# A 512-byte load put ahead of the first store of an interleaving copy kernel

## The chip, the cores and the metric

The kernel runs on one core of a Trainium2 chip. The metric is the device time of one execution in microseconds (us). Before the change its median over three runs is 314.22 us. Besides these runs there is one profiled execution, whose trace gives every instruction, the issue and landing of every transfer, and the packets of the core's 16 DMA engines.

## The reference: what is computed

Two float32 arrays `x` and `y` of shape (32, 256, 1024), 33.55 MB each, are woven together along the last axis into one array of shape (32, 256, 2048), 67.11 MB:

```python
result = np.zeros((batch, seq, dim * 2), dtype=np.float32)
result[..., 0::2] = x
result[..., 1::2] = y
```

There is no arithmetic. Every input byte is read from HBM once and every output byte is written to HBM once, 134.22 MB in all.

## The kernel before

All arrays are taken flat. With P = 128 partitions and W = 8192 elements, `x` and `y` fall into n = 8 steps of 128 x 8192 elements (4 MB each, 32 KB to a partition), and the output into 8 steps of 128 x 16384. Each output step is made and stored in two halves h = 0, 1 of 128 x 8192. There are two tiles each of `xt`, `yt` (input, by the parity of the step k) and `ot` (output, by the half h), 32 KB to a partition each.

Three engines share the work, each with an order written out by hand:

- **SP's queue (q1 in the profile) loads.** Line 45 loads the first half of x of step 0. After that it loads y of step 0 (line 55), then x (line 52) and y (line 55) of each following step. The loads of steps 0 and 1 wait for nothing. From step 2 on, a load waits until VectorE has read the tile that it overwrites (lines 50 and 54, the semaphore `woven`, which counts finished copies).
- **VectorE (DVE) weaves.** For each half, line 67 copies a half of `xt` into the even columns of `ot[h]`, and line 70 a half of `yt` into the odd columns. From step 1 on, line 66 makes it wait until the store that last read `ot[h]` has landed (`osem[h]`).
- **ACT's queue (q10) loads once and stores.** Line 46 loads the second half of x of step 0 (semaphore `hsem`). Lines 72 to 78 then store each half when both of its copies are done (line 74). A store moves 4 MB. The very first one is issued in two pieces of 1 MB and 3 MB (`parts`, with Q = W/4); both are counted by `osem[0]`, and line 66 waits for both before step 1.

`tile_interleave_kernel` also moves the first load of SP and of ACT (lines 45 and 46) to the front of the program, ahead of its opening barrier. At the end ACT waits for the last store of half 0 (line 80) and clears the semaphores in one range (line 83), and SP waits for the last store of half 1 (line 84). That last wait ends the span.

All loads of SP's queue and all stores of ACT's queue run on the same 16 DMA engines.

Of the kernel before, what the change touches and what calls it, by code (L numbers as in the profile page):

```python
# [3 lines left out]


def _interleave(nc, x, y, out):
    P = 128
    W = 8192
    H = W // 2  # L10

    total = 1
    for s in x.shape:
        total *= s
    n = total // (P * W)
    assert n * P * W == total

    def rows(ap, names, k):
        flat = ap.rearrange("b s d -> (b s d)")
        return flat[k * names : (k + 1) * names].rearrange("(p w) -> p w", p=P)  # L20

    fp32 = mybir.dt.float32
    xt = [nc.alloc_sbuf_tensor(f"xt{b}", [P, W], fp32).ap() for b in (0, 1)]
    yt = [nc.alloc_sbuf_tensor(f"yt{b}", [P, W], fp32).ap() for b in (0, 1)]
    ot = [nc.alloc_sbuf_tensor(f"ot{b}", [P, W], fp32).ap() for b in (0, 1)]

    xsem = [nc.alloc_semaphore(f"xsem{b}") for b in (0, 1)]
    hsem = nc.alloc_semaphore("hsem")
    ysem = [nc.alloc_semaphore(f"ysem{b}") for b in (0, 1)]
    woven = nc.alloc_semaphore("woven")  # L30
    osem = [nc.alloc_semaphore(f"osem{b}") for b in (0, 1)]

    xs = [rows(x, P * W, k) for k in range(n)]
    ys = [rows(y, P * W, k) for k in range(n)]
    os_ = [rows(out, 2 * P * W, k) for k in range(n)]

    Q = W // 4

    def parts(k, h):
        return [slice(0, W)] if k or h else [slice(0, Q), slice(Q, W)]  # L40

    def stored(k, h):
        return 16 * sum(len(parts(j, h)) for j in range(k))

    nc.sync.dma_start(out=xt[0][:, :H], in_=xs[0][:, :H]).then_inc(xsem[0], 16)
    nc.scalar.dma_start(out=xt[0][:, H:], in_=xs[0][:, H:]).then_inc(hsem, 16)
    for k in range(n):
        b = k % 2
        if k >= 2:
            nc.sync.wait_ge(woven, 4 * (k - 2) + 3)  # L50
        if k:
            nc.sync.dma_start(out=xt[b], in_=xs[k]).then_inc(xsem[b], 16)
        if k >= 2:
            nc.sync.wait_ge(woven, 4 * (k - 2) + 4)
        nc.sync.dma_start(out=yt[b], in_=ys[k]).then_inc(ysem[b], 16)

    for k in range(n):
        b = k % 2
        for h in (0, 1):
            c = slice(h * H, (h + 1) * H)  # L60
            if h == 0:
                nc.vector.wait_ge(xsem[b], 16 * (k // 2 + 1))
            elif k == 0:
                nc.vector.wait_ge(hsem, 16)
            if k:
                nc.vector.wait_ge(osem[h], stored(k, h))
            nc.vector.tensor_copy(out=ot[h][:, 0::2], in_=xt[b][:, c]).then_inc(woven, 1)  # L67
            if h == 0:
                nc.vector.wait_ge(ysem[b], 16 * (k // 2 + 1))
            nc.vector.tensor_copy(out=ot[h][:, 1::2], in_=yt[b][:, c]).then_inc(woven, 1)  # L70

    for k in range(n):
        for h in (0, 1):
            nc.scalar.wait_ge(woven, 4 * k + 2 * h + 2)
            for c in parts(k, h):
                nc.scalar.dma_start(
                    out=os_[k][:, h * W : (h + 1) * W][:, c], in_=ot[h][:, c]
                ).then_inc(osem[h], 16)

    nc.scalar.wait_ge(osem[0], stored(n, 0))  # L80
    used = sorted(s.num for s in [*xsem, hsem, *ysem, woven, osem[0]])
    assert used == list(range(used[0], used[-1] + 1)), used
    nc.scalar.sem_clear(range(used[0], used[-1] + 1))
    nc.sync.nop(nofuse=True).wait_op(osem[1], stored(n, 1), "sem-ge").then_inc(
        osem[1], -stored(n, 1)
    )


def kernel(tc, x, y, out):
    nc = tc.nc  # L90
    tc.close()
    tc.compile()

    _interleave(nc, x, y, out)

    blocks = nc.main_func.blocks
    for engine in (mybir.EngineType.SP, mybir.EngineType.Activation):
        opening = blocks[0].instructions
        at, moved = next(
            (b, i)  # L100
            for b in blocks[1:]
            for i in b.instructions
            if i.engine == engine and i.opcode == "DMACopy"
        )
        assert not (moved.sync_info and moved.sync_info.on_wait)
        body = at.instructions
        body.remove(moved)
        gate = next(
            n
            for n, i in enumerate(opening)  # L110
            if i.engine == engine and i.opcode == "Drain"
        )
        opening.insert(gate, moved)
        at.instructions = body
        blocks[0].instructions = opening


# [1 line left out]
_INS = ['x', 'y']  # L119
_OUTS = [((32, 256, 2048), 'float32')]  # L120


# [23 lines left out]
```

## Time and profile before

| What | Value |
|---|---|
| Runs before: median, lowest, highest | 314.22, 314.08, 314.38 us |
| Profiled execution: own time, span | 314.21 us, 312.9 us (312.88) |
| Bytes moved | 134.22 MB, mean 429 GB/s over the span |
| DMA packets' time, share of 16 engines' span | q1 48.5%, q10 51.3% |
| DVE busy | 71.9 us (23%), 32 copies of about 2.29 us |
| Load of y of step 0 landed | 22.00 us |
| First store issued, its two pieces landed | 24.35 us; 40.4 and 57.5 us |
| x and y of step 1 (issued at 1.95 and 2.48 us) landed | 32.9 and 46.9 us |
| Last store issued, landed | 298.04 us, 312.85 us |

The span runs from the first to the last instruction of the profiled execution. The execution's own time is 1.33 us longer, which lies around the span. Rates in the windows view are the bytes of the packets that start in a window, divided by its length; so a window gives a true rate only where it holds whole packets. TensorE does nothing here, and the columns of its clock can be passed over.

### The profile page before, as it was taken

To read this page: it belongs to the slowest core of one execution; us is meant where nothing else is said; L and a number is where in the kernel's file an instruction comes from. 1 tells how busy PE (TensorE), PEld (TensorE's weight loads), DVE (VectorE), ACT (ScalarE), POOL (GpSimd) and SP (SyncE) were. 2 spreads that over 40 slices of the span, in tenths; PEclk is the share of its full clock that TensorE was granted. 3 is DMA by queue.
4 is the path that set the end of the run, shared out by engine and by line. 5 is a ranking of instruction groups with operands and counts; after the bars stand their busy time and mean duration, and the time that the engine had idled before them with its cause. 6 is when DMAs were issued, how large, how long until landed. Compare 5 with 4: busy or idle time off the path is not lost.

```text
span 312.9 us, 114 instructions
## 1 busy us (share of the span) xinstructions
DVE 71.9 (23%) x32; POOL 0.2 (0%) x4
## 2 busy tenths in 40 slices
DVE  0216000501305023050230503205032050415400
POOL 0000000000000000000000000000000000000000
DMA  8999999999999999999999999999999999999998
GB/s 344 461 406 431 436 402 431 440 465 406 448 423 431 440 406 465 402 469 402 469 402 465 406 457 415 436 436 419 452 402 469 402 469 402 469 402 461 411 444 360
DMA packets 4896, 134.22 MB, mean 429 GB/s; under 512 B 544, under 2 KB 544, under 8 KB 544
## 3 DMA queue, kind: packets, MB, share of 16 engines
q10 hardware_dynamic: 2592, 69.21, 51.3%
q1 hardware_dynamic: 2304, 65.01, 48.5%
HBM read 67.11 MB, written 67.11 MB: 429 GB/s over the span
## 4 chain that ended last, share of the span: by engine, by line
DMA 82%; DVE 12%; issue 0%
DMA out_dram<-ot 76%; DMA yt<-in_y_dram 7%; DVE ot L70 6%; DVE ot L67 6%
## 5 line engine op out<-in xcount | busy, mean ns | idle before, releaser
L67 DVE COPY ot<-xt 128x4096 f32<-128x4096 f32 x16 | 36.7, 2295 | 218.0 <-DMA out_dram<-ot 206.3
L70 DVE COPY ot<-yt 128x4096 f32<-128x4096 f32 x16 | 36.6, 2288 | 8.0 <-DMA yt<-in_y_dram 8.0
L130 POOL MEMSET const-uint8-127<- 128x1 uint8 x1 | 0.1, 102 | 0.0
L130 POOL MEMSET const-bfloat16-1.0<- 128x1 bf16 x1 | 0.1, 101 | 0.0
L130 POOL MEMSET const-float32-0.0<- 128x1 f32 x1 | 0.1, 98 | 0.2 <-issue 0.2
L130 POOL MEMSET const-float32-1.0<- 128x1 f32 x1 | 0.1, 98 | 0.0
## 6 DMA issues: line engine op xcount, KB each, us to landing
out_dram<-ot ACTq DMA_DIRECT2D x15, 4096.0 KB, 34.1
yt<-in_y_dram SPq DMA_DIRECT2D x8, 4096.0 KB, 41.5
xt<-in_x_dram SPq DMA_DIRECT2D x7, 4096.0 KB, 24.4
out_dram<-ot ACTq DMA_DIRECT2D x1, 3072.0 KB, 32.8
xt<-in_x_dram SPq DMA_DIRECT2D x1, 2048.0 KB, 11.7
xt<-in_x_dram ACTq DMA_DIRECT2D x1, 2048.0 KB, 13.4
out_dram<-ot ACTq DMA_DIRECT2D x1, 1024.0 KB, 16.1
```

The lines of the kernel that those rows point to most:

```text
L67: nc.vector.tensor_copy(out=ot[h][:, 0::2], in_=xt[b][:, c]).then_inc(woven, 1)
L70: nc.vector.tensor_copy(out=ot[h][:, 1::2], in_=yt[b][:, c]).then_inc(woven, 1)
L130: nc = _bacc.Bacc("TRN2", target_bir_lowering=False, num_devices=1)
```

## The change

ACT issues one more DMA directly ahead of the first store, behind the same wait on `woven`. It loads 8 rows of 16 float32 (64 bytes each, 512 bytes in all) from step 0 of x into a new tile `spare`, which nothing reads. Its semaphore `tsem` is waited for after ACT's last store was issued, and it is cleared with the others.

```diff
+    spare = nc.alloc_sbuf_tensor("spare", [8, 16], fp32).ap()
...
     hsem = nc.alloc_semaphore("hsem")
+    tsem = nc.alloc_semaphore("tsem")
...
     for k in range(n):
         for h in (0, 1):
             nc.scalar.wait_ge(woven, 4 * k + 2 * h + 2)
+            if k == h == 0:
+                nc.scalar.dma_start(out=spare, in_=xs[0][:8, :16]).then_inc(tsem, 16)
             for c in parts(k, h):
                 nc.scalar.dma_start(
                     out=os_[k][:, h * W : (h + 1) * W][:, c], in_=ot[h][:, c]
                 ).then_inc(osem[h], 16)

+    nc.scalar.wait_ge(tsem, 16)
     nc.scalar.wait_ge(osem[0], stored(n, 0))
-    used = sorted(s.num for s in [*xsem, hsem, *ysem, woven, osem[0]])
+    used = sorted(s.num for s in [*xsem, hsem, tsem, *ysem, woven, osem[0]])
```

## The prediction

> **What bounds the kernel now.** I read the page first, for which resource is full.
>
> ```profile
> span 312.9 us, 114 instructions
> DVE 71.9 (23%) x32; POOL 0.2 (0%) x4
> DMA  8999999999999999999999999999999999999998
> q10 hardware_dynamic: 2592, 69.21, 51.3%
> q1 hardware_dynamic: 2304, 65.01, 48.5%
> ```
>
> The packets of the two queues fill 51.3 + 48.5 = 99.8% of the time of 16 DMA engines, and the third line has no slice below 8 tenths. VectorE is idle three quarters of the time. So the 16 engines bound the kernel, from the start to the end.
>
> The chain of waits names stores at 76% of the span. That is not a latency that could be cut: each of its long pieces is a store that shares the engines with loads. Its steady part gives the rate.
>
> ```profile
> 1.57 20.43 DMA yt<-in_y_dram
> ...
> 81.37 34.17 DMA out_dram<-ot
> 115.54 0.02 issue
> 115.57 2.29 DVE ot L67
> ...
> 154.29 2.29 DVE ot L67
> ...
> 193.03 2.29 DVE ot L67
> ```
>
> The columns are start, length and what. One step takes 154.29 - 115.57 = 38.72 us and 193.03 - 154.29 = 38.74 us. It moves 16.78 MB, so 433 GB/s. The windows view (length, VectorE, POOL, clock, DMA share, GB/s) tells whether the mixture matters. I chose edges just ahead of the starts of packets.
>
> ```profile
> 14.93:27.05 12.12, 5.03 (x3) 0.00 (x0) 1.00 1.00 433
> 27.05:39.69 12.64, 1.67 (x1) 0.00 (x0) 1.00 1.00 415
> 44.00:54.60 10.60, 0.00 (x0) 0.00 (x0) 1.00 1.00 433
> 284.00:310.60 26.60, 8.89 (x4) 0.00 (x0) 1.00 1.00 434
> ```
>
> Loads alone (first row), loads with stores (third) and stores alone (fourth) run at 433, 433 and 434 GB/s, whatever VectorE does beside them. Only the second row is lower. It begins with the first packets of the first store, the very place of the change: 415 against 433 over 12.64 us at a DMA share of 1.00, so its packets take longer. This costs 12.64 x (1 - 415/433) = 0.53 us. The packet records put it on loads of 32 KB, which took 1.23 to 1.59 us instead of 1.213 in the first three turns that alternate with store packets, and again, smaller, where the 3 MB piece begins.
>
> **A ceiling on any gain.** The change acts from 24.4 us on. At 22.00 us (1.57 + 20.43) y of step 0 had landed, 8.39 MB in all; 125.83 MB were left. At 433.3 GB/s they need 290.4 us; the span used 312.88 - 22.00 = 290.88. So a perfect remainder would save 0.48 us (0.15%), and that is nearly all the slow stretch above. The other losses, engines idle for the first microsecond and slow first packets, lie before 22.00.
>
> **The change part by part.** I count against the profiled execution's own 314.21 us (312.88 of span and 1.33 around it), 0.01 below the median of the runs.
>
> *One more issue on ACT.* A DMA issue takes 0.338 to 0.456 us in the stores' row:
>
> ```profile
> L76 ACTq DMA_DIRECT2D out_dram<-ot x17: 338/338/456, 24.4 to 298.0; - x17
> ```
>
> The load takes over the wait on `woven`, so it is issued at 24.35 and the 1 MB piece some 0.37 us later (24.72), the 3 MB piece at about 25.1. The third store waits for a copy until 28.75 anyway. Nothing else is queued behind the load on ACT, and SP's and POOL's instructions are not passed. The cover is q1: x and y of step 1, issued at 1.95 and 2.48, keep the engines full until they land at 32.9 and 46.9. What the stores lose in turns the loads gain. Cost: 0. Without cover it would be 0.34 to 0.46 us.
>
> *Its packets.* 512 bytes at 433 GB/s are 0.001 us. The trace has no data packet of 64 bytes. The nearest rows are the 4-byte packets that end every transfer, 6 to 9 ns each, with the next packet right behind them. The fixed part of a data packet, from 309 ns for 8 KB and 1213 ns for 32 KB, is about 8 ns. One engine gets one row if eight engines share the load and eight rows if one does, and one closing packet: 2 to 9 packets, 0.02 to 0.08 us. From above: packets of 16 KB at the very start, with no transfer ahead of them, took 0.95 to 1.58 us where 0.611 is usual, so an exposed read costs up to 0.97 us. From below: where it moves turns out of the slow stretch, it can save up to 0.48. I take 0.02, because in full flow a load packet behind another takes 1.213 us without a gap, and this one always stands behind another. The Trainium skill, page "DMA: Bandwidth & Descriptors", section "Why a DMA increments its semaphore by 16 and not by 1", says that eight rows go to the eight lowest-numbered engines, one row each; no run here shows it yet, and the sum would be the same 0.02.
>
> *Turns.* In the records q1 and q10 alternate by packet on an engine, and a 4-byte packet takes a turn of its own. So an engine that got a row spends up to two turns of q10 on tiny packets, and its first store packet comes up to two load packets (2.4 us) later than on the others. Store and load progress then differ between engines by that much, but every engine still has the same bytes to move. The next link is VectorE's wait for both pieces (57.5 us), which may move to about 60. Its store, issued at 62.13, would move to 64.5, and q10 is occupied by the second half's store until 76.8. At the end, the last two stores are issued at 288.42 and 298.04 while the store ahead lands at 293.49 and 303.18: some 5 us of cover each. Cost: 0.
>
> *The late wait and the clear.* ACT waits for `tsem` after the last issue at 298.04, some 270 us after the load; the range clear takes one more semaphore, 63 ns, at 303.2, where 312.85 sets the end. Cost: 0.
>
> Sum: 314.21 + 0.00 + 0.02 = 314.23, with the slow stretch open by up to half a microsecond either way. Since engines with a row meet the stretch later, and it ends with x of step 1, I lean a trifle down: 314.2 us.
>
> **The rivals.** About 0.2% (0.63 us, beside a spread of the runs of 0.30) is what a measurement of this kernel can tell from no change.
>
> *The slow stretch goes.* If it comes of all 16 engines beginning their stores at the same time, or of q10's first packet, the load dissolves it. For: it stands nowhere else. Against: only part of the engines change, and the slowest one sets the end. 314.21 - 0.48 = 313.7. Only together with the spread of the final landings (312.53 to 312.85, 0.32 us) could it pass 0.63. Chance 0.13, of which 0.05 beyond 0.2%.
>
> *The tiny load stalls its engines (slower).* If an engine lets nothing follow until the 64 bytes have come from HBM, both queues stand on it, and q1 is no cover. Price: the exposed part above, 0.34 (945 - 611 ns) to 0.97 us: up to 315.2; it decides from 0.63 on, two thirds of the way. Against: the closing packets pass without a gap. Chance 0.12 of over 0.63. The same page, section "Anatomy of one DMA", gives a fixed cost of about 2.0 us to each DMA, nearly all of it completion. If that stood in series on an engine, the time would be an estimated 316.2; the 4-byte packets, which take 6 to 9 ns, speak against it.
>
> *The slow stretch lasts longer (slower).* If tiny packets and shifted turns spread it, the rate of its first 4.95 us (381 in the windows view) could hold until the 1 MB piece lands at 40.4: (40.4 - 32.0) x (1 - 381/433) = 1.0 us, 315.2. Chance 0.06.
>
> *It does not act as written,* say the store is issued first: 314.2, chance 0.02.
>
> **How the numbers follow.** The forecast, no change that can be told, has 0.67. With 0.08 of the first rival and 0.02 of the last, within 0.2% comes to 0.77; faster 0.05; slower 0.12 + 0.06 = 0.18. The range starts at the ceiling on gains, 313.7, and reaches to 315.0, into the two slower rivals; beyond it lies little over 1 in 10.
>
> **What would show it.** Right: the packets under 512 B grow by 16 to 24 from 544, the first store is issued near 24.7, the two pieces land later by up to 2.4 us, a step still takes 38.7 us, and the rate from 27 to 40 us stays near 415. A rate near 433 there shows the first rival; packets of over 2 us beside the load, or a DMA share below 1, the second; a low rate past 33 us the third. A step other than 38.7 us would make the argument wrong as a whole, since I hold that no mixture changes the engines' rate.

## The result and the profile after

The changed kernel takes 315.23 us (median of 6 runs, 314.87 to 315.90), the kernel before 314.21 us beside it (6 runs, 314.08 to 314.38). The ratio is 1.0034, 95% interval 1.0021 to 1.0047. So the change costs 1.0 us, and the forecast of no change, with 315.0 as the upper end, was wrong. The changed kernel also spreads more, 1.0 us against 0.3. Its profiled execution took 314.87 us with a span of 313.54, 0.66 above the span before, and is the fastest of the six; some of the median's loss is therefore in no profile of it.

The page after, its lines that answer to those of before:

```profile
span 313.5 us, 116 instructions
DMA packets 4912, 134.22 MB, mean 428 GB/s; under 512 B 560, under 2 KB 560, under 8 KB 560
q10 hardware_dynamic: 2608, 69.21, 51.2%
q1 hardware_dynamic: 2304, 65.01, 48.6%
```

The load added 16 small packets (544 to 560): eight of 64 bytes and eight closing ones (the 4-byte packets that end a transfer). So eight engines take part, one row each. In the trace the load's semaphore rises once at 24.98 us and then eight times from 30.13 to 30.37. That agrees with what the Trainium skill, page "DMA: Bandwidth & Descriptors", section "Why a DMA increments its semaphore by 16 and not by 1", says: the sequencer writes the count of the engines that take no part at once, and each of the others adds one when its share has landed.

The timeline after, around the change (start, length, engine, line; L55 and L58 are the loads of x and y, L81 the store):

```profile
24.35 0.54 ACTq L79 DMA_DIRECT2D spare<-in_x_dram  x1
24.92 4.19 ACTq L81 DMA_DIRECT2D out_dram<-ot  x3
...
26.54 0.33 SPq L55 DMA_DIRECT2D xt<-in_x_dram  x1
```

The issue took 0.54 us, more than any store's, and the first store went out at 24.92 instead of 24.35.

The chain of waits after, two steps of it:

```profile
154.95 2.29 DVE ot L70
...
193.67 2.30 DVE ot L70
```

A step is still 38.72 us. So the loss does not lie in this part. To find the place I read the windows view in a way that depends little on the edges: GB/s divided by the DMA share is the speed of the packets that start in a window, and 433 is normal. Before, from 27 to 38, from 38 to 50 and from 110 to 310 us (length, VectorE, POOL, clock, DMA share, GB/s):

```profile
27.00:38.00 11.00, 1.72 (x1) 0.00 (x0) 1.00 1.01 417
38.00:50.00 12.00, 0.00 (x0) 0.00 (x0) 1.00 1.02 437
110.00:310.00 200.00, 49.47 (x22) 0.00 (x0) 1.00 1.01 435
```

After:

```profile
27.00:38.00 11.00, 1.72 (x1) 0.00 (x0) 1.00 1.03 434
38.00:50.00 12.00, 0.00 (x0) 0.00 (x0) 1.00 1.00 406
110.00:310.00 200.00, 49.47 (x22) 0.00 (x0) 1.00 1.00 433
```

The first stretch became better (417/1.01 = 413 before, 434/1.03 = 421 after), the second worse (428 before, 406 after), and the rest is as it was. The second one narrows down to 0.6 us. Its bytes tell how many packets of 32 KB start in it: 874 GB/s x 0.6 us are 16, 819 are 15. The share gives how long they take. First before, then after:

```profile
41.90:42.50 0.60, 0.00 (x0) 0.00 (x0) 1.00 2.04 874
```

```profile
41.90:42.50 0.60, 0.00 (x0) 0.00 (x0) 1.00 2.80 819
```

Before, 2.04 x 16 x 0.6 / 16 = 1.22 us each, the usual 1.21. After, 2.80 x 16 x 0.6 / 15 = 1.79 us. The packet records show which they are: loads of y of step 1. The records carry no number of an engine, but a packet begins within a few ns of the end of the one ahead of it on its engine, so they can be strung into 16 chains. By these, seven engines without a row have finished the 1 MB piece at 39.8 to 39.9 us, have sent their first packet of the 3 MB piece, and then have a load of 1.94 to 2.08 us. (The eighth without a row had a slow load earlier, 1.57 us at 39.87, and finished at 41.4.) The engines with a row finish the 1 MB piece at 42.0 to 42.3, and the load right behind its closing packet takes mostly 1.6 us.

By the packet records, the time that packets of over 1 KB took beyond the usual, on average over 16 engines, was 0.47 us before and 0.19 after between 26 and 38 us, 0.06 and 0.64 between 38 and 50, 0 and 0.08 between 50 and 110, and no more than 0.01 later in either. The last store's landings on the 16 engines spread over 0.32 us before (312.53 to 312.85) and 0.61 after (312.90 to 313.51). The slowest engine sets the end: it ended 0.20 us after the mean before, and 0.33 after. Of the 0.66 us, then, -0.28 + 0.58 + 0.08 are slow packets, 0.13 is the uneven end, and of the remaining 0.15 some 0.09 arises in the first six microseconds, ahead of the change.

### The profile page after: what moved, and what is told of

It is laid out like the page before. It is cut to its first block, busy times and chain, and to the rows that moved or that the text cites. A ratio compares the mean times of both kernels' runs of the same rounds, so it can differ in the third digit from the quotient of the medians.

```text
span 313.5 us, 116 instructions
## 1 busy us (share of the span) xinstructions
DVE 72.0 (23%) x32; POOL 0.2 (0%) x4
## 4 chain that ended last, share of the span: by engine, by line
DMA 77%; DVE 12%; another core or an unknown queue 5%; ACTq 0%; issue 0%; DVEq 0%
DMA out_dram<-ot 71%; DMA yt<-in_y_dram 7%; DVE ot L73 6%; DVE ot L70 6%; ACTq L79 0%; ACTq L81 0%; DVEq L69 0%
## 6 DMA issues: line engine op xcount, KB each, us to landing
yt<-in_y_dram SPq DMA_DIRECT2D x8, 4096.0 KB, 42.3
```

## The experiments

The theories when they began: **A**, the load takes turns of the store queue from eight engines, these fall out of step with the other eight, and being out of step makes packets slow where one transfer gives way to the next. **B**, the load itself, or the later issue of the store, costs. **C**, chance: slow packets anywhere. **D** was added later: the number of turns lost costs, through a load queue that runs dry (has no packet to send). Engines are called in step when they reach the same packet of a transfer at about the same time.

**The changed kernel again.** No edit.

> The changed kernel once more, unaltered, for a second profile. Theory A (two groups): the load gives eight engines two extra turns, so they run out of step with the other eight, and where the first store's 1 MB piece gives way to the 3 MB piece one group still sends the small packets while the other sends the large ones; loads in flight there (42 to 44 us) take 1.6 to 2.1 us instead of 1.21. Then the stretch from 41 to 45 us is slow again, about 0.5 us lost, and the time is 314.8 to 315.9. Theory B (the load itself or the later issue of the store): the loss stands between 27 and 33 us, and none at 42. Theory C (chance): the slow packets stand somewhere else in the span than in the first profile.

Measured: 315.38 us, ratio 1.0035 (1.0023 to 1.0048); profiled at 315.02.

```profile
41.90:42.50 0.60, 0.00 (x0) 0.00 (x0) 1.00 2.48 819
```

The same place is slow again, 2.48 x 9.6 / 15 = 1.59 us for a load. That speaks against C. The size there differs: by the packet records 0.38 us were lost between 38 and 50 us, against 0.64 in the first profile, and 0.20 between 50 and 110. The final landings spread over 1.07 us here.

**All 16 engines instead of eight.**

```diff
-    spare = nc.alloc_sbuf_tensor("spare", [8, 16], fp32).ap()
+    spare = nc.alloc_sbuf_tensor("spare", [16, 16], fp32).ap()
...
-                nc.scalar.dma_start(out=spare, in_=xs[0][:8, :16]).then_inc(tsem, 16)
+                nc.scalar.dma_start(out=spare, in_=xs[0][:16, :16]).then_inc(tsem, 16)
```

> 16 rows instead of 8, so that each of the 16 engines gets one row and the same turns. Theory A: no engine is out of step with another, the stretch from 41 to 45 us is as before, 314.0 to 314.4 us. Theory B: the load and the later issue are the same or doubled, 315.2 us or more. Theory C: as the changed kernel, 314.8 to 315.9 with the slow packets anywhere.

Measured: 314.26 us beside 314.24, ratio 1.0005 (0.9997 to 1.0014).

```profile
41.90:42.50 0.60, 0.00 (x0) 0.00 (x0) 1.00 2.19 874
85.00:95.00 10.00, 0.00 (x0) 0.00 (x0) 1.00 0.97 419
```

A larger load with the same wait and a first store at 24.74 costs nothing that the median tells: loads at 42 us take 1.31 us. B falls, for the load and for the later issue. Not every run was free, though: four of the eleven took 314.68 to 314.87 us, above all 24 runs of the kernel before beside them (at most 314.49), and the profile is of the fastest, 314.12. The second row is for later: 419/0.97 = 432.

**One engine instead of eight.** `spare` has one row, `xs[0][:1, :16]`.

> One row instead of 8: the issue on ACT and the delay of the first store are the same, but one engine alone gets the turns. Theory A: 15 engines stay in step, the loss at 42 us is small, 314.2 to 314.5 us, unless one engine out of step is enough. Theory B: 315.2 us. Theory C: 314.8 to 315.9.

Measured: 315.49 us, ratio 1.0033 (1.0022 to 1.0043). A had said 314.2 to 314.5 us, unless one engine out of step is enough. It is enough, though the runs spread from 314.48 to 316.01 us. The profiled execution (316.01, the slowest of its runs) shows how. Fifteen engines land the last store by 313.05 us, and one at 314.66. By the packet records that engine had a store packet of 2.05 us at 84.95 and a load of 2.24 us at 95.47, in a part where no other engine had a slow one; it never caught up. The mean over the engines lost only 0.15 us more than before. What counts is the slowest engine.

**The load behind the first store.** The same two lines of code stand behind the loop over the pieces, so that the engines are in step at 42 us and out of step from 57 us on.

> The same 8-row load, issued directly behind both pieces of the first store instead of ahead of them. The engines are then in step when the 1 MB piece gives way to the 3 MB piece, and fall out of step only where the first store ends (57 us), with packets of 32 KB following. Theory A: no loss at 42 us, the slow stretch from 27 to 32 us as before the change, 314.1 to 314.4 us; if being out of step itself costs, a loss at 57 us and later. Theory B (the later issue): 314.2 us. Theory C, or the load itself: 315.2 us.

Measured: 314.55 us, ratio 1.0010 (1.0002 to 1.0019), just above the 314.1 to 314.4 of A.

```profile
41.90:42.50 0.60, 0.00 (x0) 0.00 (x0) 1.00 2.06 874
```

At 42 us all is usual (1.24 us). Slow packets stand at 85 and at 94.5 us instead (by the records, on eight engines at 94.5, with 0.3 to 0.4 us more on most of them), and the landings at the end spread over 0.50 us. So being out of step costs 0.3 us in that part too.

**Balanced: a second load on the other queue.** SP issues a load of the same shape between x and y of step 1, so that the eight engines lose as many turns of loads as of stores.

```diff
...
+        if k == 1:
+            nc.sync.dma_start(out=spare2, in_=xs[0][8:16, :16]).then_inc(usem, 16)
         nc.sync.dma_start(out=yt[b], in_=ys[k]).then_inc(ysem[b], 16)
...
```

The tile `spare2` and the semaphore `usem` are made, waited for and cleared like `spare` and `tsem`.

> The changed kernel with a second load of the same shape, on SP's queue between x and y of step 1. The same eight engines lose two turns of the store queue at 28 us and two turns of the load queue at about 32 us, so that they are in step with the others again before the 1 MB piece ends. Theory A (the cost is being out of step there): the extra load takes the loss away, no slow packets from 41 to 45 us, 314.1 to 314.5 us. Theory B (each tiny load costs by itself): 315.2 us or more, up to 316.2.

Measured: 314.45 us, ratio 1.0007 (0.9998 to 1.0015).

```profile
41.90:42.50 0.60, 0.00 (x0) 0.00 (x0) 1.00 2.02 874
```

Twice the suspect, and the loss cannot be told from nothing: 1.21 us for a load at 42 us, and landings at the end within 0.22 us. The second load takes away the lateness of the stores as well (x of step 3 is issued at 79.22 us, 79.16 before the change), but with 16 rows that lateness was there (81.53) and the median was that of the kernel before. Together the two are the strongest evidence for A.

**Balanced late.** The second load stands behind y of step 1 (`if k == 2`, ahead of SP's wait), so the engines come into step again only after 42 us.

> As the balanced kernel, but the second 8-row load stands on SP's queue behind y of step 1 instead of ahead of it, so that the eight engines come back into step at about 47 us: after the place where the pieces change (42 us), but before the load queue runs dry (81 us) and the end. It splits the loss in two. If all of it is the slow packets at 42 us, 315.2 us as the changed kernel. If all of it is what comes after 80 us and the uneven end, 314.3 us. By the first profiles (0.55 us at 42 to 45 us, 0.1 at 96 to 106, 0.1 in the uneven end) I expect the first to stay: 314.6 to 315.0 us, slow packets at 42 us, none after 80 us, and the engines ending within 0.35 us of each other.

Measured: 314.88 us, ratio 1.0022 (1.0013 to 1.0031).

```profile
41.90:42.50 0.60, 0.00 (x0) 0.00 (x0) 1.00 2.54 819
```

The slow loads at 42 us are there (1.63 us), and after 50 us only two packets are slow, by 0.2 us at most. That accounts for about 0.6 us of the changed kernel's 1.0. The rest would come after, as with the load behind the first store. The split is rough, since the two intervals overlap (1.0013 to 1.0031 here, 1.0021 to 1.0047 there). One expectation failed: the landings at the end spread over 0.88 us and not 0.35. So what is unequal at the end arises at 42 us, where the two groups lose unequally, and stays.

**Early.** The 8-row load is issued right behind ACT's first load, where there are no stores beside it.

> The same 8-row load, issued on ACT's queue right behind the first load, some 23 us ahead of the first store. Its turns are spent at about 13 us, where there are no stores, so that no engine is out of step by more than the few ns of the packets, and the first store is issued on time. Theory A: 314.1 to 314.4 us, no slow packets from 41 to 45 us. Theory B (the load itself): 315.2 us.

Measured: 314.19 us, ratio 0.9996 (0.9987 to 1.0005); 1.22 us for a load at 42 us (2.04 and 874 in the window). The load by itself, with the same eight engines, is free.

**Twice.** Two 8-row loads ahead of the first store.

> Two 8-row loads ahead of the first store instead of one, so that eight engines lose four turns of the store queue. Theory A: they are twice as far out of step (up to 4.9 us); the slow packets from 41 to 45 us stay or grow, and the engines' queues run dry at different times after 80 us; 315.2 to 316.5 us. Theory B (a cost per load): 316.2 us. If what counts is only that the engines differ, and not by how much, 315.2 us.

Measured: 318.66 us (317.37 to 319.88), ratio 1.0138 (1.0112 to 1.0164). It costs over four times as much as one load, and more than any theory said.

```profile
85.00:95.00 10.00, 0.94 (x1) 0.00 (x0) 1.00 1.04 387
```

387/1.04 = 372: most of the loss has moved to 85 to 97 us, where little was slow with one load (0.98 and 423, so 432, in the first profile of the changed kernel). The landings at the end spread over 3.4 us.

**Twice on all 16 engines.** Two 16-row loads.

> Two 16-row loads ahead of the first store: every engine loses the four turns that eight of them lost with two 8-row loads (318.7 us). Theory A (being out of step costs): all engines stay in step, 314.1 to 314.6 us, although the stores come still later and the load queue runs dry for longer after 80 us. Theory D (the number of turns lost, or the dry load queue, costs): 317 us or more, with slow packets at 85 to 96 us on all engines.

Measured: 315.83 us, ratio 1.0054 (1.0042 to 1.0067). A's number failed: these engines lose their turns alike, and yet it costs 1.6 us. D's number, 317 us or more, failed too; its place came.

```profile
80.81 2.30 DVE L72 COPY ot<-xt 128x4096 f32<-128x4096 f32 x1 [14.88 <-DMA out_dram<-ot]
83.02 2.29 DVE L75 COPY ot<-yt 128x4096 f32<-128x4096 f32 x1
83.13 0.33 SPq L57 DMA_DIRECT2D xt<-in_x_dram  x1
```

```profile
85.00:95.00 10.00, 0.31 (x1) 0.00 (x0) 1.00 0.95 351
```

The first fence is its timeline, the second its windows view. x of step 3 is issued at 83.13 us because it waits for the copy that waits for the late store; y of step 2 had landed at 80.62. By the packet records no engine had a packet of a load between 80.3 and 88.0 us. When the loads came back the packets were slow on all engines until 95 us (351/0.95 = 369). With one load on 16 engines x of step 3 was issued at 81.53, y of step 2 landed at 81.66, loads were back from 85.8 on, and nothing was slow (432). So D fits as a second cost, with a point from which it counts between these two; no run changes the empty time alone, so it is argued and not shown. In the kernel before, x of step 3 is issued at 79.16 and y of step 2 lands at 84.14, and the load queue does not run dry there. The issue in the kernel before, and in the changed one:

```profile
79.16 0.33 SPq L52 DMA_DIRECT2D xt<-in_x_dram  x1
```

```profile
81.63 0.33 SPq L55 DMA_DIRECT2D xt<-in_x_dram  x1
```

One thing here speaks against A as the whole cause at 42 us: the doubled 16-row kernel, whose 1 MB piece lands within 0.5 us on all engines (43.7 to 44.2), also lost 0.38 us by the packet records between 38 and 50 us, as much as the second profile of the changed kernel.

**The first store in one piece, without and with the load.**

```diff
-        return [slice(0, W)] if k or h else [slice(0, Q), slice(Q, W)]
+        return [slice(0, W)]
```

> The kernel before with its first store in one piece of 4 MB instead of 1 MB and 3 MB, without the load; to be compared with the same kernel with the load. No change of pieces at 40 us, so nothing slow at 39 to 41 us; whether the first store's slow stretch from 27 to 32 us is the same is not known. 314.0 to 315.0 us.

> The 8-row load ahead of a first store in one piece of 4 MB (without the load: 314.5 us). Theory A: eight engines are out of step by up to 2.4 us, so it is slower than without the load; the slow packets stand where the first store gives way to the second (57 to 62 us) or after 80 us, and none at 42 us; 314.8 to 316 us. If the loss needs the change from small to large packets, it is 314.5 us, as without the load.

Measured: 314.52 us without (ratio to before 1.0009, 1.0000 to 1.0018) and 315.09 with (1.0028, 1.0018 to 1.0039), in two series. The windows view, without and then with:

```profile
27.00:38.00 11.00, 1.65 (x1) 0.00 (x0) 1.00 1.04 423
```

```profile
27.00:38.00 11.00, 1.77 (x1) 0.00 (x0) 1.00 0.99 381
```

The load costs 0.57 us here as well, so the loss does not need the change from small to large packets. The place was not the one that A expected: the start of the stores itself is slower (385 against 407), and nothing later. Yet the engines stay out of step: a store's shares land some 2.6 us apart on them until 283 us, while the rate is 433.

```profile
110.00:310.00 200.00, 49.03 (x22) 0.00 (x0) 1.00 1.00 433
```

So being out of step does not by itself make packets slow; A holds only for certain places.

**The kernel before again.** No edit.

> The kernel before once more, for a second profile. If the slow stretch from 27 to 32 us belongs to the start of the stores, it is there again with 0.4 to 0.6 us lost, and less than 0.1 us is lost after 33 us; 314.1 to 314.4 us.

Measured: 314.30 us in its one run. By the packet records 0.39 us were lost between 26 and 38 us, and 0.19 between 38 and 50, twice what was expected there. So these stretches differ by 0.1 us and more from profile to profile, and the 0.28 us that the changed kernel's profile gained at 27 us may be partly that.

No version beat the kernel before.

## Why the prediction was wrong

**The ceiling on gains** stood: no kernel was faster by what can be told.

**The issue on ACT** was mis-sized, 0.54 us against 0.37, but it is hidden as predicted: in the balanced kernel the issue takes 0.55 us, the first store goes out at 24.90, and the time cannot be told from that before.

**The packets** cost what was said. The ones of 64 bytes took 11 ns each in the records, with the next packet right behind; the early load (314.19) bears it out. So the rival of the stalling load is false. The Trainium skill, page "DMA: Bandwidth & Descriptors", section "Anatomy of one DMA", gives a fixed cost of about 2.0 us, fitted there to DMAs that GpSimd issues and put down mostly to completion. It does not stand in series on an engine here.

**The turns, "Cost: 0", is the step that failed.** Their mechanism was predicted as it came: the engines with a row ran up to 2.4 us late with their stores (the 1 MB piece landed at 40.1 to 41.7 on one group and at 42.4 to 42.6 on the other). But I concluded that the same bytes at the same rate end at the same time. The rates of 433 in the windows that I compared were those of engines in step. Out of step the steady part still ran at 433, but where the 1 MB piece gave way to the 3 MB piece the loads took 1.4 to 2.1 us. The sum was also one of means, while the end is set by the slowest engine. I put 0 where the times of the runs show some 1.0 us: about 0.6 with the engines out of step up to 46 us only (balanced late), and 0.3 to 0.4 after it. How it divides is less firm than the sum, since the two profiles of the changed kernel lost 0.64 and 0.38 us between 38 and 50.

**The cover was followed along the wrong queue.** I checked that stores were always pending, and not that the late store delays the copy that releases x of step 3 (79.16 to 81.63 us). In the changed kernel this costs little (with 16 rows x of step 3 is as late, 81.53 us, and the median did not move); in the two doubled kernels most of the slow packets stand where the loads come back.

**The lean to less** saw the first stretch rightly (0.47 to 0.19 us), within what profiles differ by, and missed that the loss would come back at the next change of transfer. The prediction had read slow loads there in the trace before, "again, smaller, where the 3 MB piece begins", and then wrote of the slow stretch that "it stands nowhere else". No rival was built on that place, where the loss came.

**Nearest was the third rival,** "tiny packets and shifted turns spread it", 315.2 us, which had 0.06. That its price agrees with the measured 315.23 is luck: it was worked out for a low rate up to 40.4 us, while the stretch from 27 us lost less and a new one opened at 42.

**What stays open:** why loads become slow when some engines are a packet or two ahead of others, and only at some places where a transfer or a queue begins (27, 42, 85 and 94 us) and never after 110 us, although a store's shares land some 1.8 us apart on the engines of the changed kernel until 271 us. No run looked below the packet. Also open is how the unprofiled runs of up to 315.9 us divide.

## What to carry to other kernels

A transfer with fewer rows than engines is not small because its bytes are few: on a queue shared by turns it moves some engines behind the others, and the slowest one sets the end. In this kernel it was free in a place where no store was beside it, and nearly free with as many rows as there are engines; two of these cost 1.6 us. When a store is delayed behind cover, follow what its landing releases, up to the next load, and see whether that load queue still has work.

## What was not expected of the hardware

- One engine of 16 out of step costs as much as eight: a median of 315.49 us against 315.23, from runs of 314.48 to 316.01.
- The loss grows faster than the number of turns: 1.0 us for one 8-row load, 4.4 us for two (318.66 against 314.30).
- Issuing the 8-row DMA took 543 ns and the 16-row one 354, while the issue of a store of 4 MB mostly takes 338. A second 8-row one right behind the first took 290.
- A load queue that was empty for about 8 us came back with slow packets on all 16 engines (369 of 433 GB/s for 10 us); after under 5 us empty, with one 16-row load, it came back with none.
